# One decoder step on one core: the scheduler of the attention stage follows a model of the vector engines' queues, and the weights of a prompt tile's two heads are scaled on two engines

## The chip, the cores and the metric

One core of a Trainium2 chip. The metric is the device time of one execution in microseconds. The kernel before takes 830.26 us (median of three runs, 829.99 to 830.6).

## The reference

One inference step of one decoder layer, for a prompt of 512 tokens and a sample group of 8 sequences with 8 new tokens each (576 tokens in all) that share the weights. A combined projection (1024 to 3584 columns) feeds two groups of 8 heads of 64: retention with group norm and gate, and dilated window attention. Then one output projection, a gated feed-forward with a short convolution (2816 wide), residuals and norms.

```python
proj = _rmsnorm(x, norm1_w) @ w_in
rq, rk, rv, rg, aq, ak, av = jnp.split(proj, points, axis=-1)
ro, ret_s = _retention(rq, rk, rv, ret_s0)
ro = jax.nn.silu(rg) * groupnorm(ro)
k_all, v_all = concat([win_k, ak]), concat([win_v, av])
ao = _dilated_attention(aq, pos, k_all, v_all, k_start)   # softmax over (128,1),(512,4),(2048,16)
x = x + concat([ro, ao]) @ w_out
ua, ub = jnp.split(_rmsnorm(x, norm2_w) @ w_up, [D_FF], axis=-1)
x = x + (jax.nn.silu(causal_conv(ua)) * ub) @ w_down
y = _rmsnorm(x, normf_w)
```

The prompt has no cached keys; each sample sequence has 1024 cached rows, of which the kernel reads 768.

## The kernel before, in words

**Tiles.** Activations are kept transposed, 128 features by 576 tokens. A weight chunk is 128 output columns by up to 8 blocks of 128 inputs. Each is split by ScalarE into a rounded part (`whi`, L219) and by VectorE into the rest (`wlo`, L229), so that three products of fast matmuls give nearly full precision. A *dense step* is one such block: six matmuls of 288 columns (L254), into a PSUM tile `d`. There are two `d` tiles, and four smaller PSUM tiles `m`.

**Stages.** Load and norm; retention, with the input projection beside it (to about 150 us); attention, again with the input projection beside it (150 to 334 us); then output projection and feed-forward, dense steps only.

**The order of the work.** `Merge` writes the instruction streams of all engines in one pass, while the kernel is built. Each part of the work is a Python generator, which issues some instructions and then yields how long TensorE is taken, how long it wants to rest before its next piece, and how much of its budget it has used. `Merge` keeps a clock of TensorE's work. It resumes the generator that is due, those without a budget first, then the one that is furthest behind its budget; if none is due, the clock jumps. The rests are fixed numbers, written by hand. Each engine then executes its instructions in the order in which they were issued.

**The generators of the attention stage.**
- `in_proj` (budget 130 us): for each of the 28 column blocks it takes a `d` tile, issues its eight dense steps, and adds `in_post`, which evicts `d` on VectorE (L527 to L563). The last four blocks are retention's gates; their activation (L529) is ScalarE's, with a table load of its own, and the product with the retention result `roT` (L533) is POOL's, VectorE's for the last.
- `attn_prompt` and `attn_unit`: four head pairs, four query tiles each. A tile: the queries rounded and split (L756 to L760); scores of the two heads (L769, L771) into two `m` tiles; bias and running minimum on VectorE (`s`, L779); exponential and sum on ScalarE (L786); a reciprocal on VectorE (L789); the weights of both heads scaled on POOL (L791); transposes (L797), their evictions (`pt`, L801), and the products with the values (L810).
- `attn_sample` and `unit`: eight units of four sequences. Keys are transposed (L883) and copied by VectorE and ScalarE (`kt`, L884); POOL copies the new keys to their end (L982); scores (L893) go to a `d` tile in two halves of 512 and 264 columns, of which only the second needs the new keys; bias (L900), exponential (L905), reciprocal and scaling on VectorE (L907, L908, L910); transposes into another `d` tile (L916, L917), evictions (`spt`, L920, L921), products (L928), a copy (`ob`, L937), a transpose (L943) and two copies into `aoT` (L946).
- `mix_split` rounds and splits each finished block of `aoT` and `roT` for the output projection (L1017, L1019).

**Room in PSUM.** `room(n)` lets a generator wait until n of the four `m` tiles are free by its own count; `give(n)` frees them when the eviction has been issued, not when it is done. `d` tiles are taken without a question. The pools make the instructions wait for real, whatever the scheduler believes.

Of the kernel before, what the change touches and what calls it, by code (L numbers as in the profile page):

```python
# [94 lines left out]

class Merge:
# [7 lines left out]
    def __init__(self):  # L104
        self.clock, self.live, self.n = 0.0, [], 0

# [3 lines left out]
    def add(self, gen, left=None, delay=0.0):  # L110
        self.n += 1
        self.live.append({"g": gen, "left": left, "vt": self.floor(), "at": self.clock + delay, "n": self.n,
                          "stuck": False})

    def run(self, until=None):
        while self.live and not (until and until()):
            free = [e for e in self.live if not e["stuck"]]
            assert free, "every stream waits"
            ok = [e for e in free if e["at"] <= self.clock]
            if ok:  # L120
                e = min(ok, key=lambda e: (e["left"] is not None, e["vt"] if e["left"] else e["at"], e["n"]))
            else:
                e = min(free, key=lambda e: (e["at"], e["n"]))
                self.clock = e["at"]
            try:
# [21 lines left out]
def decoder_step(ctx, tc, a):  # L147
    nc = tc.nc
    pe, dve, act, pool, sp = nc.tensor, nc.vector, nc.scalar, nc.gpsimd, nc.sync
# [12 lines left out]
    def room(n):  # L162

        while held[0] + n > 4:
            yield None
        held[0] += n

    def give(n):
        held[0] -= n

    def dtile():
        return psd.tile([P, 1024], F32, name="d", tag="d")
# [155 lines left out]
    mg = Merge()  # L328
# [193 lines left out]
    def in_post(m, ps):  # L522
        sec, hp = m // 4, m % 4
        y = tok(ps)
        if sec == 3:
            t = atp.tile([P, T], F32, name="t3", tag="t6", bufs=1)
            dve.tensor_mul(t, y, rstd_b)  # L527
            yield 0.0, 800.0
# [6 lines left out]
        elif sec < 4:  # L535
# [4 lines left out]
            dve.tensor_mul(t, y, kds.pop(hp) if sec == 1 else rstd_b)  # L540
            if m in first:
                evac.append(m)
# [10 lines left out]
        else:  # L553
            r = A.setdefault(hp, {})
            t = atp.tile([P, T], F32, name=f"t{sec}", tag=f"t{sec}", bufs=1 if sec == 6 else 2)
            if sec == 4:
                dve.scalar_tensor_tensor(t, y, -(DH ** -0.5), rstd_b, op0=OP.mult, op1=OP.mult)  # L557
                yield 0.0, 2300.0
# [3 lines left out]
            else:  # L562
                dve.tensor_mul(t, y, rstd_b)  # L563
                yield 0.0, 1700.0
# [11 lines left out]
    def in_proj():  # L576
        for m in IN_ORDER:
# [3 lines left out]
            else:  # L581
                while hp > 1 and (sec < 3 and ret_done[0] < hp - 1 or sec > 3 and used.get(hp - 2, 0) < 6):
                    yield None
                ps = dtile()
# [159 lines left out]
    def attn_unit(hp, i):  # L744
# [111 lines left out]
    def attn_sample():  # L856
# [31 lines left out]
        def unit(u):  # L888
            hp, g = units[u]
            ps = dtile()  # L890
# [4 lines left out]
            for x in range(4):  # L895
# [5 lines left out]
                                     op1=OP.min, accum_out=c[:, 0:1])  # L901
            if g == 1 and hp < 3:
# [10 lines left out]
            yield 0.0, 1100.0  # L913
            ps = dtile()
# [6 lines left out]
            act.copy(pt[:, 3:7].rearrange("p j q -> p (j q)"), ps[:, 384:KEYS + P])  # L921
            yield 0.0, 2200.0
# [65 lines left out]
    mg.add(in_proj(), 130.0e3)  # L988
# [13 lines left out]
    rpx.close()  # L1002

# [18 lines left out]
    mg.run()  # L1022
    mid.close()
# [308 lines left out]
```

## Time and profile before

| | |
|---|---|
| median of 3 runs | 830.26 us |
| the profiled execution | 830.02 us |
| its span, first to last instruction | 828.2 us |
| TensorE busy | 809.3 us (98%) |
| VectorE, ScalarE, POOL busy | 413.4 (50%), 294.4 (36%), 148.0 us (18%) |
| granted TensorE clock, mean | 0.997 |
| DMA | 128.67 MB, 155 GB/s over the span |

Busy TensorE is not TensorE at its peak: the end of a matmul is modelled, and matmuls overlap in the record, so a short wait can lie inside a busy stretch. An idle row names who ended the wait. A row of a group gives the busy time, the mean of one instruction in ns, and the idle time ahead of it. Names like `s` or `d` are the program's tiles, without their numbers.

### The profile page before, as it was taken

How to read it: one execution, taken by the hardware profiler on the slowest of the kernel's cores; microseconds unless marked ns; L12 is line 12 of the kernel's file. 1: busy time of each engine (PE TensorE's matmuls, PEld its weight loads, DVE VectorE, ACT ScalarE, POOL GpSimd, SP SyncE). 2: the span in 40 equal slices, each digit the busy share in tenths (PEclk: the TensorE clock that was granted, in tenths of full speed). 3: DMA queues.
4: the chain of work that ended last, by engine and by line, in shares of the span. 5: the costliest groups of instructions: out<-in, count | busy, mean ns of one | idle time of the engine just before them, and what ended most of it. 6: DMA issues, size and time to landing. Idle time of an engine off the chain costs nothing.

```text
span 828.2 us, 15913 instructions
## 1 busy us (share of the span) xinstructions
PE 809.3 (98%) x6559; PEld 772.3 (93%) x6559; DVE 413.4 (50%) x792; ACT 294.4 (36%) x503; POOL 148.0 (18%) x240
## 2 busy tenths in 40 slices
PE   7999999999999999999999999999999999999995
PEld 5999999887887888999999999999999999999995
DVE  4664555665546566743545545432245545443333
ACT  5422222454535567433223323311123323332222
POOL 1321202111110213032122322100012322310111
PEclk9999999999999999999999999999999999999998
DMA  9354753678786863456255554443334455543213
GB/s 265 105 175 115 213 173 101 184 210 226 213 254 185 228 177 91 111 185 197 77 179 178 178 187 160 124 137 91 96 99 161 145 153 179 172 160 93 71 52 115
DMA packets 179798, 128.67 MB, mean 155 GB/s; under 512 B 14976, under 2 KB 176400, under 8 KB 179213
## 3 DMA queue, kind: packets, MB, share of 16 engines
q1 hardware_dynamic: 178573, 93.75, 40.4%
q10 hardware_dynamic: 928, 33.63, 11.3%
q8 instruction: 52, 0.85, 0.4%
q0 software_dynamic: 224, 0.28, 0.1%
q14 instruction: 21, 0.17, 0.1%
HBM read 121.52 MB, written 39.66 MB: 195 GB/s over the span
## 4 chain that ended last, share of the span: by engine, by line
PE 93%; ACT 3%; DVE 1%; issue 1%; DMA 1%; POOL 0%; SPq 0%; ACTq 0%; DVEq 0%
PE d L254 74%; PE m L883 2%; PE d L451 2%; PE m L928 1%; PE d L893 1%; PE m L810 1%; PE m L797 1%; PE m L496 1%; PE m L1222 1%; PE px L254 1%; PE m L666 1%; DMA wraw<-in_w_in_dram 1%; ACT s L786 1%; PE m L630 1%; PE px L410 1%
## 5 line engine op out<-in xcount | busy, mean ns | idle before, releaser
L219 ACT ACTIVATE whi<-wraw 128x1024 fp32r<-128x1024 f32 (+2 forms) x114 | 110.5, 970 | 369.2 <-issue 182.6
L229 DVE TENSOR_TENSOR wlo<-wraw,whi 128x1024 fp32r<-128x1024 f32 (+2 forms) x114 | 127.1, 1115 | 121.7 <-ACT whi L219 118.9
L254 PE MATMUL d<-bhi,whi 128*128 128x288 f32 x768 | 172.7, 306 | 1.2 <-DVE t L557 1.2
L254 PE MATMUL d<-bhi,wlo 128*128 128x288 f32 x768 | 164.2, 295 | 0.0
L254 PE MATMUL d<-blo,whi 128*128 128x288 f32 x768 | 163.9, 295 | 0.0
L254 PE MATMUL d<-hhi,whi 128*128 128x288 f32 x704 | 151.0, 296 | 0.0
L254 PE MATMUL d<-hlo,whi 128*128 128x288 f32 x704 | 150.8, 296 | 0.0
L254 PE MATMUL d<-hhi,wlo 128*128 128x288 f32 x704 | 150.7, 296 | 0.0
L254 PEld LDWEIGHTS d<-bhi,whi 128*128 128x128 f32 x768 | 121.7, 189 | 6.3 <-issue 3.1
L254 PEld LDWEIGHTS d<-bhi,wlo 128*128 128x128 f32 x768 | 123.3, 188 | 0.0
L254 PEld LDWEIGHTS d<-blo,whi 128*128 128x128 f32 x768 | 123.2, 188 | 0.0
L254 PEld LDWEIGHTS d<-hhi,whi 128*128 128x128 f32 x704 | 113.5, 189 | 0.1
L254 PEld LDWEIGHTS d<-hhi,wlo 128*128 128x128 f32 x704 | 113.5, 189 | 0.0
L254 PEld LDWEIGHTS d<-hlo,whi 128*128 128x128 f32 x704 | 113.5, 189 | 0.0
L1130 DVE TENSOR_TENSOR ue<-d,rstd_b 128x512 f32<-128x512 f32 x22 | 15.2, 691 | 74.5 <-PE d L254 74.5
L1149 POOL TENSOR_TENSOR g<-g,cv 128x512 f32<-128x512 f32 x20 | 25.8, 1289 | 142.2 <-DVE g L1146 136.7
L791 POOL TENSOR_SCALAR s<-s,sc 128x128 f32<-128x128 f32 (+3 forms) x32 | 17.3, 549 | 140.5 <-DVE sc L789 125.9
L1046 POOL TENSOR_TENSOR acc<-acc,sq 128x576 f32<-128x576 f32 x13 | 20.9, 1611 | 104.2 <-ACT sq L1045 104.2
L1135 POOL COPY cout<-ue 128x2 f32<-128x2 f32 x22 | 5.7, 260 | 137.6 <-DVE ue L1130 137.6
L884 ACT COPY kt<-m 128x384 f32<-128x384 f32 x32 | 15.3, 479 | 38.4 <-PE m L883 36.2
L883 PE MATMUL m<-ident,kc 128*128 128x128 f32 x192 | 27.4, 277 | 0.8 <-DVE sc L779 0.7
L884 DVE COPY kt<-m 128x384 f32<-128x384 f32 x32 | 17.8, 556 | 19.4 <-PE m L883 19.0
(269 smaller groups left out, 1027.3 us busy)
## 6 DMA issues: line engine op xcount, KB each, us to landing
wraw<-in_w_up_dram SPq DMA_DIRECT2D x44, 512.0 KB, 4.7
wraw<-in_w_in_dram SPq DMA_DIRECT2D x26, 512.0 KB, 3.8
kc<-in_cache_win_k_dram SPq DMA_DIRECT2D x32, 256.0 KB, 4.8
vc<-in_cache_win_v_dram SPq DMA_DIRECT2D x32, 256.0 KB, 3.2
wraw<-in_w_down_dram SPq DMA_DIRECT2D x16, 384.0 KB, 4.0
wraw<-in_w_down_dram SPq DMA_DIRECT2D x16, 320.0 KB, 3.2
kc<-in_cache_win_k_dram SPq DMA_DIRECT2D x64, 64.0 KB, 3.4
vc<-in_cache_win_v_dram SPq DMA_DIRECT2D x64, 64.0 KB, 3.3
```

The source lines that it names most:

```text
L219: act.activation(split[i][0][:, c], raw[i][:, c], AF.Copy)
L229: dve.tensor_sub(lo[:, c], raw[i][:, c], f32(hi[:, c]))
L254: pe.matmul(ps[:, C0 + s * H2:C0 + (s + 1) * H2], wt[:, rows[k] if rows else k - k0], x[k][:, s * H2:(s + 1) * H2], start=first and k == k ...
L410: pe.transpose(ps[:, s], xn[:r, j, k * P:(k + 1) * P], ident[:r, :r])
L451: pe.matmul(ps[i][:, C0 + s * H2:C0 + (s + 1) * H2], wt[:, k], x[k][:, s * H2:(s + 1) * H2], start=k == 0 and wt is hi and x is xhis, stop ...
L496: pe.transpose(p1[:, j * P:(j + 1) * P], src[:, j * P:(j + 1) * P], ident)
L791: pool.tensor_scalar(s[:, :n], s[:, :n], c[:, 2:3], 1.0, op0=OP.mult, op1=OP.mult)
L883: pe.transpose(ps[:, j * P:(j + 1) * P], K[u, x][:, 3 * w + j], ident)
L884: (act.copy if w else dve.tensor_copy)(kt[:, w * 384:w * 384 + 384], ps[:, :384])
L1046: pool.tensor_tensor(acc, acc, sq, op=OP.add)
L1130: dve.tensor_mul(u[:, 2:NP + 2], ya[:, :NP], rstd_b[:, :NP])
L1149: eng.tensor_tensor(g[:, :NP], g[:, :NP], c[:, :NP], op=OP.mult)
```

## The change

`Queues` keeps, for VectorE, ScalarE and POOL, a modelled time at which each would be done with all that was issued to it: a fixed part and a part per element for each instruction. `Engine` wraps the three engines, so that each instruction is noted there. In the attention stage (`follow`):
- a generator other than `in_proj` is not due again before the latest modelled end of what it just issued, plus 150 ns, whatever its own rest says;
- `give(n)` frees `m` tiles at that modelled end, and `room` waits for it;
- a `d` tile is taken only when the last but one has been read, by the model (`dgive`, `droom`).

Apart from the scheduler, the scaling of the weights of a prompt tile's second head goes to VectorE, the first head's stays on POOL, and the rest behind it is shorter.

```diff
+class Queues:
+    COST = {"dve": (130.0, 1.1), "act": (150.0, 0.87), "pool": (250.0, 1.0)}
...
+    def note(self, name, op, out):
+        base, each = self.COST[name]
+        n = math.prod(out.shape[1:])
+        if name == "pool" and op == "tensor_tensor":
+            each = 2.4
+        t = max(self.clock[name], self.now) + base + n * each
+        self.clock[name] = t
+        self.end = max(self.end, t)
...
             self.clock += c[0]
             e["at"] = self.clock + c[1]
+            if self.follow and not e["dense"]:
+                e["at"] = max(e["at"], self.queues.end + 150.0)
...
     def room(n):
-        while held[0] + n > 4:
-            yield None
+        while True:
+            while freed and freed[0][0] <= mg.clock:
+                held[0] -= freed.pop(0)[1]
+            if held[0] + n <= 4:
+                break
+            yield (0.0, max(freed[0][0] - mg.clock, 10.0)) if freed else None
         held[0] += n
...
     def give(n):
-        held[0] -= n
+        if mg.follow:
+            freed.append((queues.end, n))
+            freed.sort()
+        else:
+            held[0] -= n
...
+    def dgive(ps):
+        read[id(ps)] = queues.end
...
+    def droom():
+        while mg.follow and len(large) > 1:
+            t = read.get(id(large[-2]))
+            if t is not None and t <= mg.clock:
+                break
+            yield None if t is None else (0.0, max(t - mg.clock, 10.0))
...
-        for ps, s, c in S:
-            pool.tensor_scalar(s[:, :n], s[:, :n], c[:, 2:3], 1.0, op0=OP.mult, op1=OP.mult)
-        yield 0.0, 2.5 * n + 300.0
+        for eng, (ps, s, c) in zip((pool, dve), S):
+            eng.tensor_scalar(s[:, :n], s[:, :n], c[:, 2:3], 1.0, op0=OP.mult, op1=OP.mult)
+        yield 0.0, 1.25 * n + 500.0
...
-    mg.add(in_proj(), 130.0e3)
+    mg.add(in_proj(), 130.0e3, dense=True)
...
     mg.run(lambda: fin_ret)
     rpx.close()
+    mg.follow = True
```

`dgive(ps)` stands behind each instruction that reads a `d` tile for the last time, `yield from droom()` ahead of each `dtile()` of the input projection and of the sample's units. The stage up to the end of retention is issued as before. `order` rows of the changed kernel carry its own line numbers: L328 is L254 of before, L876 L797, L889 L810, L962 L883, L973 L893, L998 and L999 L916 and L917, L1011 L928, L1026 L943, and every instruction of the three wrapped engines has L131.

**Place 1: TensorE's order at the first head pair's last prompt tile.** Before, from the key transposes behind the scores of the sample's unit (which stand a few rows earlier) to the transposes of its weights:

```order
L883 MATMUL m<-ident,kc 128x128 x6
L254 MATMUL d<-bhi,whi 128x288 x2
L254 MATMUL d<-blo,whi 128x288 x2
L254 MATMUL d<-bhi,wlo 128x288 x2
L810 MATMUL m<-pt,n_1724 64x128 x8
L883 MATMUL m<-ident,kc 128x128 x6
L254 MATMUL d<-bhi,whi 128x288 x2
L254 MATMUL d<-blo,whi 128x288 x2
L254 MATMUL d<-bhi,wlo 128x288 x2
L916 MATMUL d<-ident,ss 128x128 x6
L917 MATMUL d<-ident,ss 128x128
```

and now:

```order
L962 MATMUL m<-ident,kc 128x128 x6
L973 MATMUL d<-kt,qb_404 32x512 x4
L973 MATMUL d<-kt,qb_404 32x264 x4
L570 MATMUL m<-ident,t_2230 128x128 x4
L571 MATMUL m<-ident,t_2230 128x128
L962 MATMUL m<-ident,kc 128x128 x6
L876 MATMUL m<-ident,s 128x128 x8
L998 MATMUL d<-ident,ss 128x128 x6
L999 MATMUL d<-ident,ss 128x128
```

Three dense steps stood between these groups, two of them in the rows shown; now there is none between the scores and the transposes of the weights (`d` from `ss`).

ScalarE's order there, now (`s` the prompt tile's weights, `n` the next pair's value tile, `kdec` and `ka` the next pair's keys, `ss` the sample's weights):

```order
L131 COPY kt<-m 128x384
L131 ACTIVATE s,sc<-s,sc 128x512 x2
L131 COPY n_2254<-m 128x512
L131 CAST kdec<-t_1846 64x512
L131 CAST ka_2285<-t_1846 64x512
L131 ACTIVATE ss,ssc<-ss,ssc 128x776
```

The eviction of the value tile and the casts of the next pair's keys stand between the prompt's exponentials and the sample's.

**Place 2: VectorE and POOL at the last head pair's last prompt tile.** VectorE, before, from the tile's last score pass on (`s` its scores, `sc` their sums):

```order
L779 ISA s,sc<-m,pb 128x512
L779 ISA sc 128x1
L920 COPY spt<-d 128x384
L789 RECIPROCAL sc<-sc 128x1 x2
L527 TENSOR_TENSOR t_4208<-d,rstd_b 128x576
L801 COPY pt<-m 128x512
L229 TENSOR_TENSOR wlo<-wraw,whi 128x1024
```

and now, from the eviction of a dense tile (`t`) behind its score passes on:

```order
L131 TENSOR_TENSOR t_4147<-d,rstd_b 128x576
L131 COPY kt<-m 128x384
L131 TENSOR_TENSOR wlo<-wraw,whi 128x1024
L131 RECIPROCAL sc<-sc 128x1 x2
L131 TENSOR_SCALAR s<-s,sc 128x512
```

The reciprocals stood ahead of the next split of weights (`wlo`) and now stand behind it. That split needs `whi`, and ScalarE's queue there is now: copy of `kt`, table load, the tile's two exponentials, `whi`, table load. POOL, before:

```order
L791 TENSOR_SCALAR s<-s,sc 128x384 x2
L982 COPY kt<-t_3178 128x8 x4
L533 TENSOR_TENSOR roT<-roT,t_4106 128x576
L791 TENSOR_SCALAR s<-s,sc 128x512 x2
L533 TENSOR_TENSOR roT<-roT,t_4208 128x576
```

and now:

```order
L131 TENSOR_TENSOR roT<-roT,t_3954 128x576
L131 TENSOR_SCALAR s<-s,sc 128x512
L131 COPY kt<-t_3214 128x8 x4
L131 TENSOR_TENSOR roT<-roT,t_4147 128x576
L131 MEMSET ue_4348 128x2
```

The copies of the new keys (`kt`) stood ahead of the last tile's scaling and now stand behind it.

**Place 3: the end of the attention stage.** TensorE, before, the last rows up to the last transpose of the stage:

```order
L928 MATMUL m<-n_3740,spt 32x128 x4
L254 MATMUL d<-bhi,whi 128x288 x2
L254 MATMUL d<-blo,whi 128x288 x2
L254 MATMUL d<-bhi,wlo 128x288 x2
L810 MATMUL m<-pt,n_3740 64x128 x8
L254 MATMUL d<-bhi,whi 128x288 x2
L254 MATMUL d<-blo,whi 128x288 x2
L254 MATMUL d<-bhi,wlo 128x288 x2
L254 MATMUL d<-bhi,whi 128x288 x2
L254 MATMUL d<-blo,whi 128x288 x2
L254 MATMUL d<-bhi,wlo 128x288 x2
L943 MATMUL m<-ident,ob 128x128
```

and now, with the first matmuls of the output projection at the end:

```order
L328 MATMUL d<-bhi,whi 128x288 x2
L328 MATMUL d<-blo,whi 128x288 x2
L328 MATMUL d<-bhi,wlo 128x288 x2
L889 MATMUL m<-pt,n_3623 64x128 x8
L998 MATMUL d<-ident,ss 128x128 x6
L999 MATMUL d<-ident,ss 128x128
L1011 MATMUL m<-vc,spt 32x128 x24
L1011 MATMUL m<-n_3623,spt 32x128 x4
L1026 MATMUL m<-ident,ob 128x128
L328 MATMUL d<-bhi,whi 128x288 x2
```

The last dense steps of the input projection now stand ahead of the last five groups of attention, none between them. VectorE, before, ahead of the last eviction `spt`:

```order
L907 RECIPROCAL ssc<-ssc 128x1
L908 TENSOR_SCALAR ss<-ss,ssc 128x776
L910 TENSOR_TENSOR ss<-ss,small 128x64
L779 ISA s,sc<-m,pb 128x512
L779 ISA sc 128x1
L779 ISA s,sc<-m,pb 128x512
L779 ISA sc 128x1
L920 COPY spt<-d 128x384
```

and now:

```order
L131 TENSOR_TENSOR blo<-aoT,bhi 128x576
L131 TENSOR_TENSOR t_4263<-d,rstd_b 128x576
L131 TENSOR_TENSOR blo<-aoT,bhi 128x576
L131 RECIPROCAL ssc<-ssc 128x1
L131 TENSOR_SCALAR ss<-ss,ssc 128x776
L131 TENSOR_TENSOR ss<-ss,small 128x64
L131 TENSOR_TENSOR roT<-roT,t_4263 128x576
L131 COPY spt<-d 128x384
```

The eviction of the last dense tile and a split now stand ahead of the sample's reciprocal and scaling, and the last product with `roT` ahead of `spt`.

## Rows read from the trace of the kernel before

**Rows 1.** Stages: busy us of each engine (instructions), clock, DMA share, GB/s.

```profile
core 0: us, PE busy (x) PEld busy (x) DVE busy (x) ACT busy (x) POOL busy (x), PEclk, DMA share, GB/s
...
150.00:334.00 184.00, 179.98 (x1796) 155.80 (x1796) 108.01 (x277) 100.64 (x237) 29.13 (x76) 1.00 0.71 199
334.00:400.00 66.00, 66.00 (x500) 65.80 (x498) 34.38 (x52) 23.07 (x29) 12.99 (x10) 1.00 0.53 157
400.00:500.00 100.00, 100.00 (x750) 99.93 (x751) 49.51 (x67) 32.44 (x40) 24.41 (x42) 1.00 0.53 168
500.00:800.00 300.00, 300.00 (x2263) 299.98 (x2262) 126.64 (x169) 84.70 (x107) 47.73 (x69) 1.00 0.42 129
```

**Rows 2.** Waits of TensorE's weight loads, 150 to 334 us: total, times, longest.

```profile
PEld d L893 <- POOL kt L982: 2.1, 3, 1.5
PEld m L797 <- POOL s L791: 1.9, 7, 0.5
PEld m L883 <- DVE sc L779: 1.7, 4, 0.9
...
PEld d L254 <- DVE t L557: 1.5, 1, 1.5
```

**Rows 3.** The page's groups of instructions: busy us, mean ns | idle us before.

```profile
L883 PE MATMUL m<-ident,kc 128*128 128x128 f32 x192 | 27.4, 277 | 0.8 <-DVE sc L779 0.7
```

**Rows 4.** The chain that ended last: start us, us, what.

```profile
159.26 0.81 PE m L883 x6
...
163.89 1.44 PE d L893 x16
...
192.17 1.02 PE m L810 x16
```

**Rows 5.** ScalarE's groups by shape, 150 to 334 us.

```profile
L884 ACT COPY kt<-m 128x384 f32<-128x384 f32 x32 | 15.3, 479 | 38.4 <-PE m L883 36.2 <-PE m L943 1.1 <-POOL s L791 0.6
L219 ACT ACTIVATE whi<-wraw 128x1024 fp32r<-128x1024 f32 x13 | 13.7, 1057 | 6.1 <-PE d L254 6.0
L905 ACT ACTIVATE ss<-ss,ssc 128x776 f32<-128x776 f32 x8 | 7.6, 946 | 4.2 <-DVE ssc L900 4.1
...
L786 ACT ACTIVATE s<-s,sc 128x512 f32<-128x512 f32 x8 | 5.7, 718 | 1.0 <-DVE sc L779 1.0
...
L499 ACT COPY n<-m 128x512 f32<-128x512 f32 x7 | 4.1, 588 | 12.6 <-PE m L496 12.6
...
L529 ACT ACT_TABLE_LOAD x3 | 3.8, 1283 | 0.1
...
L937 ACT COPY ob<-m 128x128 f32<-128x128 f32 x8 | 2.2, 270 | 2.3 <-PE m L928 2.3
L529 ACT ACTIVATE t<-t 128x576 f32<-128x576 f32 x3 | 2.1, 684 | 0.0
```

**Rows 6.** The timeline, pieces of three stretches: start us, us, what [idle before].

```profile
161.41 0.18 ACT L786 ACTIVATION_READ_ACCUMULATOR s<-s,sc 128x1 f32 x1
...
161.63 0.16 DVE L789 RECIPROCAL sc<-sc 128x1 f32<-128x1 f32 x1 [0.35 <-ACT s L786]
...
161.98 0.72 POOL L791 TENSOR_SCALAR s<-s,sc 128x128 f32<-128x128 f32 x2 [16.05 <-DVE sc L789]
...
186.13 1.67 DVE L229 TENSOR_TENSOR wlo<-wraw,whi 128x1024 fp32r<-128x1024 f32 x1 [0.79 <-ACT whi L219]
...
302.96 1.28 ACT L529 ACT_TABLE_LOAD   x1
...
304.25 0.68 ACT L529 ACTIVATE t<-t 128x576 f32<-128x576 f32 x1
```

**Rows 7.** VectorE's and POOL's groups by shape, 150 to 334 us.

```profile
L229 DVE TENSOR_TENSOR wlo<-wraw,whi 128x1024 fp32r<-128x1024 f32 x13 | 16.3, 1255 | 2.2 <-ACT whi L219 2.0
...
L563 DVE TENSOR_TENSOR t<-d,rstd_b 128x576 f32<-128x576 f32 x7 | 5.3, 754 | 5.7 <-PE d L254 5.6
L908 DVE TENSOR_SCALAR ss<-ss,ssc 128x776 f32<-128x776 f32 x8 | 5.0, 625 | 0.3
L920 DVE COPY spt<-d 128x384 f32<-128x384 f32 x8 | 4.5, 556 | 3.2 <-PE d L917 3.1
...
L982 POOL COPY kt<-t 128x8 f32<-128x8 f32 x32 | 5.5, 220 | 0.1
L791 POOL TENSOR_SCALAR s<-s,sc 128x512 f32<-128x512 f32 x8 | 5.5, 697 | 29.6 <-DVE sc L789 17.9 <-PE d L916 11.7
```

More of the change, by code (lines that the diff above doesn't have):

```diff
@@ L93, in _constants, with __init__, step, __getattr__ @@
     return {"c_ident": ident.astype(f), "c_small": small, "c_kdec": kdec, "c_pbias": pb, "c_sbias": sb.astype(f)}
+class Queues:
+    COST = {"dve": (130.0, 1.1), "act": (150.0, 0.87), "pool": (250.0, 1.0)}
+    def __init__(self):
+        self.clock = dict.fromkeys(self.COST, 0.0)
+        self.now, self.end = 0.0, 0.0
+    def step(self, now):
+        self.now, self.end = now, now
+    def note(self, name, op, out):
[6 more added lines that the diff above has]
+        self.end = max(self.end, t)
+class Engine:
+    def __init__(self, engine, name, queues):
+        self.engine, self.name, self.queues = engine, name, queues
+    def __getattr__(self, op):
+        f = getattr(self.engine, op)
+        if op == "dma_start":
+            return f
+        def call(*args, **kw):
+            r = f(*args, **kw)
+            self.queues.note(self.name, op, kw["out"] if "out" in kw else args[0])
+            return r
+        return call
 class Merge:
-    def __init__(self):
+    def __init__(self, queues):
         self.clock, self.live, self.n = 0.0, [], 0
+        self.queues, self.follow = queues, False
     def floor(self):
         return min([e["vt"] for e in self.live if e["left"] and not e["stuck"]], default=0.0)
-    def add(self, gen, left=None, delay=0.0):
+    def add(self, gen, left=None, delay=0.0, dense=False):
         self.n += 1
         self.live.append({"g": gen, "left": left, "vt": self.floor(), "at": self.clock + delay, "n": self.n,
-                          "stuck": False})
+                          "stuck": False, "dense": dense})
     def run(self, until=None):
@@ L124, in run @@
                 self.clock = e["at"]
+            self.queues.step(self.clock)
             try:
@@ L148, in decoder_step @@
     nc = tc.nc
-    pe, dve, act, pool, sp = nc.tensor, nc.vector, nc.scalar, nc.gpsimd, nc.sync
+    pe, sp = nc.tensor, nc.sync
+    queues = Queues()
+    dve, act, pool = (Engine(e, n, queues) for e, n in ((nc.vector, "dve"), (nc.scalar, "act"), (nc.gpsimd, "pool")))
     ctx.enter_context(tc.manual_schedule())
@@ L162, in room @@
     def room(n):
-        while held[0] + n > 4:
-            yield None
+        while True:
[4 more added lines that the diff above has]
+            yield (0.0, max(freed[0][0] - mg.clock, 10.0)) if freed else None
         held[0] += n
+    freed = []
     def give(n):
-        held[0] -= n
+        if mg.follow:
[3 more added lines that the diff above has]
+            held[0] -= n
+    large, read = [], {}
+    def dgive(ps):
[6 more added lines that the diff above has]
+            yield None if t is None else (0.0, max(t - mg.clock, 10.0))
     def dtile():
-        return psd.tile([P, 1024], F32, name="d", tag="d")
+        large.append(psd.tile([P, 1024], F32, name="d", tag="d"))
+        return large[-1]
     def f32(ap):
@@ L326, in halves @@
         return [(h2, slice(h2 * 64, h2 * 64 + 64)) for h2 in range(2)]
-    mg = Merge()
+    mg = Merge(queues)
     xhi = big.tile([P, KD, T], F32R, name="bhi", tag="bhi", bufs=1)
@@ L527, in in_post @@
             dve.tensor_mul(t, y, rstd_b)
+            dgive(ps)
             yield 0.0, 800.0
@@ L583, in in_proj @@
                     yield None
+                yield from droom()
                 ps = dtile()
@@ L889, in unit @@
             hp, g = units[u]
+            yield from droom()
             ps = dtile()
@@ L913, in unit @@
             yield 0.0, 1100.0
+            yield from droom()
             ps = dtile()
@@ L1022, in decoder_step @@
     mg.run()
+    mg.follow = False
+    held[0] = 0
     mid.close()
```

5 lines of the change are left out of this document (added).

## The prediction

> **What bounds the kernel now.** I read the stages first, then who makes TensorE wait, then the prices. The table by stage [rows 1] shows TensorE busy without a gap from 334 to 800 us; the gap before 150 us and the one after 800 us lie in parts whose order the change leaves as it is. What the change can reach is the stage from 150 to 334 us: 180.0 of 184.0 us busy, so 4.0 us idle. There TensorE alternates between pieces of attention and steps of the dense input projection (six matmuls of 288 columns), which exist to fill its waits. Its work is the same in both kernels; so the time changes by waits alone.
>
> The waits of TensorE's weight loads in that stage [rows 2] name their causes: POOL's copies of the new keys (3 waits), POOL's scaling of the weights (7), VectorE's score passes that free PSUM (4), VectorE's eviction of a dense tile (1). A matmul's shown end is modelled: a transpose of 128 columns shows 277 ns [rows 3] where six of them take 0.81 us, 0.135 each [rows 4]. Each wait therefore hides some 0.14 us more than its idle row says. **Lost now: 4.0 + 15 x 0.14 = 6.1 us.** The ends: 4.0 (the idle alone) and 7.2 (the four rows of the weight loads, counted in full).
>
> **What the change removes.** Its scheduler holds each attention piece until a model of the three vector queues says that its inputs are there, and does not begin a dense tile before the last but one has been read. All four causes are addressed, so I let 5.7 of the 6.1 us go and keep 0.4. The order shows that the attention pieces move to later places while the dense steps go on at once, so those run out earlier. New waits come from that, and I price them at the three places shown under the change, by what stands on the queues. Ends of the ranges are the same chains with nothing and with 0.19 us for every handover.
>
> **Place 1, the first head pair's last prompt tile.** Where three dense steps stood among the groups, none stands now. From the end of the key transposes (L883) to the transposes of the sample's weights (L916) TensorE has the sample's scores, 1.44 us for both halves [rows 4], five transposes of a value tile (5 x 0.135 = 0.68), six of keys (0.81) and eight of weights (1.08): 4.0 us. ScalarE meanwhile does, in its queue's order, the key copy 0.479, two exponentials of 0.718, the value copy 0.588, two casts of 512 columns (taken as that copy, 0.588 each) and the sample's exponential 0.946 [rows 5]; VectorE then a reciprocal of 0.16 [rows 6] and the scaling 0.625 [rows 7]. Sum 5.4. **Wait 1.4 us.** The second head's scaling, now on VectorE, lies beside this: no trace of before shows 128x512 there; by the 776 columns in 625 ns it is 0.41, by POOL's 0.697 at most [rows 7]; either hides behind the two casts. I take 0.41, the same engine.
>
> **Place 2, the last head pair's last prompt tile.** POOL's copies of the sample's new keys now stand on its queue behind the scaling of the last tile's first head, and the second half of the sample's scores needs them. That scaling waits for a reciprocal on VectorE, which stands behind a weight split (L229), which waits for ScalarE's weight rounding (L219), which stands behind both exponentials and, in front of them, a table load. From the end of the key transposes: copy 0.479, table load 1.283, exponentials 2 x 0.718, rounding 1.057 [rows 5], split 1.255 [rows 7], reciprocal 0.16 [rows 6], scaling 0.697, first key copy 0.220 [rows 7]: 6.6 us. Cover on TensorE: 24 dense matmuls at 100 us / 750 = 0.133 [rows 1], 3.2 us, and the first 512 of 776 columns of scores, 0.95 of 1.44: 4.1. **Wait 2.5 us**, before the second half of the scores.
>
> **Place 3, the end of the stage.** Before, three dense steps lie among the last four groups. Now the last dense step is followed by nothing but attention, five groups in one chain. (a) VectorE has an eviction of the dense tile and a split of 576 columns (0.754 each, the split taken as the eviction), the reciprocal and the scaling: 2.3 us after the last dense matmul, against 1.02 us of TensorE work (L810): wait 1.3. (b) The pack of the transposed weights (L920) now stands on VectorE behind the last gate product, which waits for ScalarE's sigmoid-weighted gate (L529) and its table load: 0.588 + 1.283 + 0.684 on ScalarE, 0.754 + 0.556 on VectorE, 3.9 us after L810; TensorE has spent 1.3 + 7 x 0.135 of it: wait 1.6. (c) The last result (L937) must be copied, 0.27, before its transpose. **Wait 3.2 us.** The output projection behind it has three steps of 0.8 us before it needs the last attention rows, and these need two small copies, a cast and a split on VectorE, the longest of them 0.754 [rows 7]: nothing.
>
> **Handovers.** The three places have 14 of them; the rows give 0.04 us from ScalarE to VectorE and 0.19 from VectorE to POOL [rows 6]. At 0.07 as a mean: 1.0 us; from 0.6 to 2.7.
>
> **Where cost is nothing.** ScalarE loads its tables seven times in the stage instead of five, 2 x 1.283 more; two of the seven are in places 2 and 3 already, the others lie under dense steps. The 16 scalings that VectorE takes over add at most 16 x 0.41 = 6.6 us to 108 busy of 184 [rows 1]; their cover is gone only where VectorE is the last of a chain, as in place 3, where none stands. On SP the loads keep their order within each tensor, and no row of the stage shows a load as a cause.
>
> **The sum.** New: 1.4 + 2.5 + 3.2 + 1.0 = 8.1 us. Gone: 5.7. Net +2.4 us: 830.02 of the profiled execution becomes 832.4, and as the median of the runs is 0.24 us above that execution, 832.7. What a measurement of this kernel can tell from no change is about 0.2%, 1.7 us.
>
> **A rule against the trace.** A table load is followed by the next activation at once: 302.96 + 1.28, then 304.25 [rows 6]. So the sum has 1.283 for each. The Trainium skill (ScalarE: Activation LUTs, What ACT_TABLE_LOAD costs) counts for each switch of tables a drain of 1380 ns beside the same 1283; by it places 2 and 3 would each be 1.4 us longer, and the time 835.5. The row does not show the drain.
>
> **Rivals.** *A, faster:* the waits end and are not replaced. In place 2 ScalarE would have to be ahead, with the table loaded before the key copy is due, and in place 3 wait (b) would have to be covered. Then new waits are 1.4 + 1.2 + 1.6 and 0.7 of handovers, 4.9, and if the weight loads' 7.2 us are all lost now and all gone, the net is -2.3: 828.0. It decides at 6.1 us of new waits. For it: the scheduler counts 738 ns for a dense step that takes 800, so real cover is larger than it believes. Against: the chains above already use the real cover. *B, no change that can be measured:* the same chains with half of place 2 and place 3's (c) hidden, +0.85: 831.1. *C, slower still:* the two engines do not scale side by side. A weight split took 1.67 us while POOL was scaling, against 1.255 in the mean [rows 6, 7], 0.41 more. If each waits for the other, the 7 waits on the scaling stay: +1.9, 834.6. The Trainium skill (SBUF — State Buffer, Who interferes with whom) has the rule for it: a VectorE scaling may take the port pair that it shares with GpSimd for the whole instruction, and the other engine blocks; the long split agrees with the section's line on instructions with two SBUF inputs. *D, a pause after each table load,* as long as the load: 2 x 1.283 in places 2 and 3, 835.3; the activation at 304.25 speaks against it. *E, the change moves nothing that TensorE waits for:* excluded, since the dense steps go at all three places.
>
> **Chances.** Forecast 0.54, A 0.11, B 0.20, C 0.13, D 0.02, E 0. The likeliest case's own range is 831.2 (6.8 us gone, handovers at 0.04) to 834.8 (3.6 us gone). Of its 0.54, some 0.04 lie under the bound of 0.2%. Slower by over 0.2%: 0.50 + 0.13 + 0.02 = 0.65; the same 0.20 + 0.04 = 0.24; faster 0.11. To leave out no more than 2 in 10 the whole takes in C and the forecast's upper end, and reaches part of the way to A: 829.3 to 835.0.
>
> **What would show it.** Right: in the changed profile TensorE waits between the two halves of the scores (d from kt) for POOL's kt copies some 15 us before the end of the stage, and before the first output-projection step it waits for VectorE's ss, for VectorE's spt and for ScalarE's ob; the chain that ended last names ScalarE's table loads there; waits of TensorE for POOL's s and for a dense eviction are gone. Wrong: TensorE without an idle row in the last 30 us of the stage, or waits of over half a microsecond that still name POOL's s.

## The result, and the profile after

The changed kernel takes 837.92 us (median of 6 runs, 836.46 to 840.19), the kernel before, run beside it, 829.67 us (6 runs, 829.06 to 830.6): ratio 1.0101, 95% interval 1.0087 to 1.0115, so 8.25 us slower. The forecast was 832.7 us with a range up to 835.0: the sign was right, the size was not. The profiled execution of the changed kernel took 840.19 us; its span is 838.4 us.

The stages of the changed kernel, columns as in [rows 1], with the time from 322 to 346 us cut finer, and a stretch at place 1:

```profile
150.00:334.00 184.00, 178.20 (x1724) 155.46 (x1723) 108.74 (x288) 99.46 (x233) 21.56 (x60) 0.98 0.71 199
197.50:200.00 2.50, 2.47 (x13) 1.92 (x13) 1.38 (x3) 0.03 (x1) 0.00 (x0) 0.50 0.98 304
322.00:329.00 7.00, 4.35 (x34) 3.27 (x32) 2.70 (x6) 6.72 (x10) 0.99 (x2) 1.00 0.04 12
329.00:334.00 5.00, 4.83 (x21) 3.34 (x22) 2.89 (x6) 1.66 (x4) 2.60 (x5) 0.66 0.00 0
334.00:337.00 3.00, 3.00 (x27) 2.83 (x27) 0.73 (x2) 1.86 (x3) 0.00 (x0) 1.00 0.00 0
337.00:342.00 5.00, 2.02 (x29) 1.55 (x29) 3.42 (x7) 2.87 (x4) 0.10 (x1) 0.87 0.01 3
342.00:346.00 4.00, 3.61 (x59) 2.98 (x52) 0.18 (x1) 1.29 (x4) 0.10 (x1) 0.50 0.40 132
...
400.00:800.00 400.00, 400.00 (x3011) 399.72 (x3010) 177.08 (x247) 116.33 (x145) 71.83 (x110) 1.00 0.45 139
```

Read two columns, TensorE's busy time and PEclk. The stage from 400 to 800 us is as full as before [rows 1]; the loss lies in the attention stage and right behind it. TensorE is idle there for 5.80 us up to 334 and 3.4 us from 334 to 346, 9.2 us where it was 4.0 before. But the granted clock, 1.00 throughout in [rows 1], is now 0.50 in 197.5:200 (place 1), 0.66 in 329:334 (place 2) and 0.50 in 342:346 (place 3): there TensorE ran at 1.2 GHz, the lower of its two levels, for part or all of the time. Ahead of all three it had stood still.

Who TensorE waited for, 150 to 346 us (total, times, longest):

```profile
PE d L973 <- POOL kt L131: 2.8, 1, 2.8
PE d L998 <- DVE ss L131: 2.3, 2, 1.4
PE m L1011 <- DVE spt L131: 1.6, 1, 1.6
PE m L876 <- DVE n L131: 0.9, 1, 0.9
PE m L876 <- DVE kt L131: 0.5, 1, 0.5
PE m L1026 <- ACT ob L131: 0.4, 1, 0.4
PE m L570 <- DVE t L131: 0.4, 1, 0.4
PE m L962 <- ACT n L131: 0.2, 1, 0.2
```

The waits of the forecast are there by name: POOL's `kt` at place 2, `ss`, `spt` and `ob` at place 3, the chain to `ss` at place 1 (0.9 of the 2.3). The `n`, `kt` and `n` rows belong to place 1 too; the forecast did not name them. No row names POOL's `s`, and none waits for a dense tile to be freed: the four causes of [rows 2] are gone outside the three places. The 0.4 us of L570 is a new one, a wait for the data of an evicted tile.

What the waits did to the work behind them is in TensorE's own timeline (start us, us, what, idle before):

```profile
189.86 0.87 PE L962 MATMUL m<-ident,kc 128*128 128x128 f32 x6
...
197.53 1.54 PE L998 MATMUL d<-ident,ss 128*128 128x128 f32 x6 [0.92 <-DVE ss L131]
...
199.95 1.46 PE L889 MATMUL m<-pt,n 128*64 128x128 f32 x16
...
325.29 1.07 PE L973 MATMUL d<-kt,qb 128*32 128x512 f32 x8
329.14 2.14 PE L973 MATMUL d<-kt,qb 128*32 128x264 f32 x8 [2.79 <-POOL kt L131]
331.21 1.97 PE L876 MATMUL m<-ident,s 128*128 128x128 f32 x8
...
336.67 1.10 PE L889 MATMUL m<-pt,n 128*64 128x128 f32 x16
...
341.70 2.79 PE L1011 MATMUL m<-vc,spt 128*32 128x128 f32 x48 [1.60 <-DVE spt L131]
```

Six transposes took 0.87 us at 189.86 and 1.54 us at 197.53, behind a wait. Sixteen products (L889) took 1.46 us at 199.95 and 1.10 at 336.67, where the clock was 1.00. In the changed kernel's chain that ended last, the 56 products of L1011 are 3.26 us long; the run below in which TensorE was kept busy has them in 1.52 and 0.40, overlapping.

### The profile page after: what moved, and what is told of

It is laid out like the page before. It is cut to its first block, busy times and chain, and to the rows that moved or that the text cites. A ratio compares the mean times of both kernels' runs of the same rounds, so it can differ in the third digit from the quotient of the medians.

```text
span 838.4 us, 15881 instructions
## 1 busy us (share of the span) xinstructions
PE 813.9 (97%) x6559; PEld 777.0 (93%) x6559; DVE 415.8 (50%) x808; ACT 297.0 (35%) x505; POOL 140.2 (17%) x224
## 4 chain that ended last, share of the span: by engine, by line
PE 95%; ACT 2%; DVE 1%; DMA 1%; issue 0%; SPq 0%; POOL 0%; ACTq 0%; DVEq 0%; POOLq 0%
PE d L328 74%; PE m L962 3%; PE d L525 2%; PE m L1011 2%; PE m L889 1%; PE d L973 1%; PE m L876 1%; PE m L570 1%; PE m L1308 1%; PE px L328 1%; DMA wraw<-in_w_in_dram 1%; PE m L745 1%; PE px L484 1%; PE m L848 1%; PE m L709 1%; ACT s L131 1%
## 5 line engine op out<-in xcount | busy, mean ns | idle before, releaser
L131 ACT ACTIVATE whi<-wraw 128x1024 fp32r<-128x1024 f32 (+2 forms) x114 | 110.6, 970 | 367.7 <-issue 186.7
L131 DVE TENSOR_TENSOR wlo<-wraw,whi 128x1024 fp32r<-128x1024 f32 (+2 forms) x114 | 126.9, 1113 | 124.4 <-ACT whi L131 121.6
L328 PE MATMUL d<-bhi,whi 128*128 128x288 f32 x768 | 173.2, 307 | 0.0
L328 PE MATMUL d<-bhi,wlo 128*128 128x288 f32 x768 | 164.5, 296 | 0.0
L328 PE MATMUL d<-blo,whi 128*128 128x288 f32 x768 | 164.4, 296 | 0.0
L328 PE MATMUL d<-hhi,whi 128*128 128x288 f32 x704 | 150.9, 296 | 0.0
L328 PE MATMUL d<-hlo,whi 128*128 128x288 f32 x704 | 150.8, 296 | 0.0
L328 PE MATMUL d<-hhi,wlo 128*128 128x288 f32 x704 | 150.7, 296 | 0.0
L328 PEld LDWEIGHTS d<-bhi,whi 128*128 128x128 f32 x768 | 122.6, 190 | 4.6 <-issue 3.0
L328 PEld LDWEIGHTS d<-blo,whi 128*128 128x128 f32 x768 | 123.9, 189 | 0.0
L328 PEld LDWEIGHTS d<-bhi,wlo 128*128 128x128 f32 x768 | 123.7, 189 | 0.0
L328 PEld LDWEIGHTS d<-hhi,whi 128*128 128x128 f32 x704 | 113.4, 189 | 0.1
L328 PEld LDWEIGHTS d<-hhi,wlo 128*128 128x128 f32 x704 | 113.4, 189 | 0.0
L328 PEld LDWEIGHTS d<-hlo,whi 128*128 128x128 f32 x704 | 113.4, 189 | 0.0
L131 DVE TENSOR_TENSOR ue<-d,rstd_b 128x512 f32<-128x512 f32 (+1 forms) x44 | 18.1, 454 | 74.6 <-PE d L328 74.6
L131 POOL TENSOR_TENSOR g<-g,cv 128x512 f32<-128x512 f32 (+1 forms) x40 | 31.2, 802 | 142.1 <-DVE g L131 136.7
L131 POOL COPY cout<-ue 128x2 f32<-128x2 f32 (+1 forms) x44 | 30.8, 730 | 137.8 <-DVE ue L131 137.8
L131 DVE TENSOR_TENSOR xT<-d,xT 128x576 f32<-128x576 f32 x23 | 17.4, 757 | 54.5 <-PE d L328 54.5
L131 POOL TENSOR_TENSOR acc<-acc,sq 128x576 f32<-128x576 f32 x13 | 21.0, 1615 | 109.6 <-ACT sq L131 109.6
L131 DVE SCALAR_TENSOR_TENSOR cv<-ue,vec,cv 128x592 f32<-128x592 f32 x44 | 36.5, 829 | 0.8
L131 POOL TENSOR_SCALAR s<-s,sc 128x128 f32<-128x128 f32 (+3 forms) x16 | 10.2, 635 | 141.0 <-DVE sc L131 114.9
L131 ACT COPY kt<-m 128x384 f32<-128x384 f32 x32 | 15.3, 478 | 47.3 <-PE m L962 45.2
```

The lines of the kernel that those rows point to most:

```text
L131: r = f(*args, **kw)
L328: pe.matmul(ps[:, C0 + s * H2:C0 + (s + 1) * H2], wt[:, rows[k] if rows else k - k0], x[k][:, s * H2:(s + 1) * H2], start=first and k == k ...
```

## The experiments

**Theory 1:** the waits came about as priced, and what the sum missed is the clock after them. **Rivals:** the waits alone, longer than priced; rival C, VectorE and POOL slowing each other in the split scaling. A second question: which half of the edit makes the loss, the scheduler or the split?

### Keeping TensorE busy in the waits

Extra matmuls whose results nothing reads stand in front of the waiting instructions.

```diff
+        def fill(ps, c0, n):
+            for _ in range(n):
+                pe.matmul(ps[:, c0:c0 + P], ident, ident, start=True, stop=True)
...
+                if u == 7 and n0:
+                    fill(ps, 800, 12)
...
+            if u in (1, 7):
+                fill(scores, 0, 4 if u == 1 else 6)
...
+            if u == 7:
+                fill(scores, 0, 7)
...
+            if u == 7:
+                fill(scores, 0, 2)
```

> The changed kernel, with extra 128x128 matmuls of the identity put in front of the matrix instructions that wait at places 1 to 3 (12 between the two halves of the last sample unit's scores, 4 or 6 before the transposes of its weights at place 1 and 3a, 7 before its products, 2 before the last small transpose). Their results are read by nothing, so the output and every wait's cause stay as they are; only TensorE is busy while it waits. Theory 1 (about 5.5 us of the 8.2 us lost are the lower level of TensorE's clock, which is granted after the new waits): the granted clock of 341.7:345.8 rises from 0.50 to near 1.00, L1011's products take about 1.7 us again instead of 3.26, and the time is 832 to 834 us. Rival (the loss is the waits themselves, with what they delay): the waits are still sat out, the time stays 837 to 839 us. Rival (split scaling slows VectorE and POOL side by side): no change either, 837 to 839 us.

Measured: 833.79 us (833.43 to 834.73, 5 runs), ratio 1.0045 (1.0033 to 1.0057) to the kernel before. Its stage, and TensorE's rows (L1021 the products):

```profile
329.00:334.00 5.00, 5.00 (x48) 4.66 (x47) 3.06 (x6) 3.74 (x6) 0.14 (x1) 1.00 0.01 3
342.00:346.00 4.00, 4.00 (x32) 4.00 (x32) 3.93 (x7) 0.00 (x0) 0.00 (x0) 1.00 0.41 100
```

```profile
328.40 1.09 PE L876 MATMUL m<-ident,s 128*128 128x128 f32 x8
...
337.63 1.52 PE L1021 MATMUL m<-vc,spt 128*32 128x128 f32 x48
338.97 0.40 PE L1021 MATMUL m<-n,spt 128*32 128x128 f32 x8
```

With more instructions to execute, the kernel is over 4 us faster: the ratio falls from 1.0101 to 1.0045, 0.56% of 830 us or 4.6 us. The eight transposes of L876 take 1.09 us instead of 1.97. Nothing that VectorE, POOL or ScalarE must do was taken away, so the two rivals are out for this part. What remains, 3.9 us, is put down to the waits; the forecast's net was 2.4. Place 1 is filled only ahead of `ss`, and its three shorter waits (0.24, 0.88 and 0.47 us) stay. Three of the five executions show a mean granted clock of 0.998 (833.4 to 833.8 us), two 0.994 (834.4 and 834.7): the filling does not keep the clock up everywhere each time.

### One place at a time

The same edit at place 3 alone, and at place 2 alone.

> The changed kernel with the unused identity matmuls at place 3 alone (6 before the transposes of the last unit's weights, 7 before its products, 2 before the last transpose). Theory 1 (the lower clock after the waits makes up what the sum missed, place by place): the products take 1.7 us again instead of 3.26, the granted clock there returns to 1.00, and 2 to 3 of the 4.1 us that the filling of all three places gave back come back: 835 to 836 us; places 1 and 2 keep a clock of 0.66 to 0.97 behind their waits. Rival (one fall at place 2 is what pulls the clock down to the end): filling place 3 changes nothing there, 837 to 838 us.

Measured: 837.21 us (836.87 to 837.75, 4 runs), ratio 1.0096 (1.0079 to 1.0113).

> The changed kernel with the 12 unused identity matmuls at place 2 alone, between the two halves of the last unit's scores. Theory 1: what follows place 2 runs at the full clock, 1 to 2 us come back, 836 to 837 us, and place 3 still shows a clock near 0.5 behind its own waits. Rival (one fall at place 2 pulls the clock down to the end): place 3 runs at 1.00 too, 834 us.

Measured: 834.31 us (833.15 to 836.02, 4 runs), ratio 1.0063 (1.0044 to 1.0081). Place 3 alone filled:

```profile
329.00:334.00 5.00, 5.00 (x23) 3.98 (x22) 2.50 (x5) 2.52 (x4) 1.58 (x2) 0.50 0.00 0
342.00:346.00 4.00, 4.00 (x64) 3.80 (x57) 2.10 (x5) 2.37 (x4) 0.10 (x1) 1.00 0.74 221
```

and place 2 alone:

```profile
329.00:334.00 5.00, 4.97 (x35) 3.79 (x35) 3.40 (x6) 2.53 (x4) 2.49 (x4) 1.00 0.01 3
334.00:337.00 3.00, 2.04 (x24) 1.62 (x22) 1.84 (x4) 1.84 (x4) 0.00 (x0) 1.00 0.00 0
337.00:342.00 5.00, 2.69 (x63) 2.19 (x63) 1.72 (x4) 2.46 (x5) 0.20 (x2) 1.00 0.27 94
```

Each filling lifts the clock where it is. The times do not follow the expected split: by the ratios place 3 gave 0.4 us, not told apart from nothing by the intervals, and place 2 gave 3.2. With place 3 filled, the profiled execution has the lower level through the whole of 329:334, the changed kernel's only in part (0.66); this may hide part of the gain. And in the second trace the waits at place 3 are all there (TensorE busy 2.04 of 3 and 2.69 of 5 us), with the clock at 1.00. So either the fall at place 2 had pulled the clock down at place 3 too, or place 3's waits bring it down in some executions only.

> The changed kernel with the unused identity matmuls at place 1 (4) and place 2 (12), and none at place 3, whose three waits (1.4, 1.6 and 0.4 us) stay. If the fall at place 2 is what brings the clock down at place 3 as well, as the run with place 2 alone filled suggests (its place 3 stood at 1.00), all of what the filling of the three places gave back comes back: 833.5 to 834.5 us, and place 3 shows 1.00. If place 3's own waits bring it down, its stretch shows about 0.5 again and the time is 835 to 836.5 us.

Measured: 835.4 us (832.2 to 835.96, 6 runs), ratio 1.0064 (1.0052 to 1.0076). The median hides two groups: the executions whose mean granted clock was 0.997 and 0.998 took 832.2 and 833.4 us, the four at 0.993 took 835.2 to 836.0. The profiled one is of the first kind, with the three waits of place 3 there and the clock up:

```profile
PE m L1019 <- DVE spt L131: 1.6, 1, 1.6
PE d L1006 <- DVE ss L131: 1.4, 1, 1.4
PE m L876 <- DVE n L131: 0.9, 1, 0.9
PE m L876 <- DVE kt L131: 0.5, 1, 0.5
PE m L1034 <- ACT ob L131: 0.4, 1, 0.4
```

```profile
334.00:337.00 3.00, 1.40 (x37) 1.14 (x38) 1.23 (x2) 1.46 (x3) 0.10 (x1) 1.00 0.12 16
```

So the clock falls in some executions of this kernel and not in others, for about 3 us of difference. Where it fell in the four others no trace shows: place 3 was left unfilled, but place 1 kept its waits for `n` and `kt`, and behind place 1's waits the clock fell in the run with place 2 alone filled (0.50 in 196:202, with places 2 and 3 at 1.00). Between the two readings this run does not decide. The first fits all three traces: place 3 fell where place 2 had fallen, and stayed up in the two in which place 2 was filled. That waits at the end of the stage can bring the clock down with no fall shortly before them is shown further down, by the scheduler alone, with a longer first wait. How much each place costs by itself is thereby not settled; the sum of the three is.

### What a wait costs by itself

In the kernel before, in the stage where TensorE has no gap, eight waits of graded length on a chain of small VectorE copies that nothing else reads:

```diff
+        n = WAITS.get(key[1], 0) if key[0] == "up" else 0
+        if n:
+            pe.matmul(ps[:64, :P], wsc, ident, start=True, stop=True)
+            for _ in range(n):
+                dve.tensor_copy(wsc, ident[:, :64])
+            pe.matmul(ps[:64, :P], wsc, ident, start=True, stop=True)
...
```

> The kernel before with eight waits put into the stretch from 400 to 700 us, where TensorE has no gap: in front of every second tile of the first feed-forward projection TensorE must wait for a chain of 1, 4, 8, 12, 2, 16, 6 and 22 small VectorE copies (64 columns, which nothing else reads); two small extra matmuls begin and end each. Theory 1: behind the longer of them (1.5 us and more) TensorE's matmuls of 288 columns take about twice their 0.133 us for some time, so these waits cost more than their length; with copies of 0.16 to 0.2 us the waits sum to 11 to 14 us, and with some 1.5 to 2 us more behind each of the four longest the time is 847 to 853 us; the short ones leave the clock at 1.00. Rival (a wait costs its length alone): 841 to 845 us and a granted clock of 1.00 throughout.

Measured: 859.87 us (858.4 and 861.35). TensorE behind two of the waits (L260 is the dense step's matmul), and the stretch behind the second in the columns of [rows 1]:

```profile
465.17 0.43 PE L254 MATMUL d<-ident,wsc 128*64 128x128 f32 x2 [1.89 <-DVE wsc L253]
465.53 0.54 PE L260 MATMUL d<-hhi,whi 128*128 128x288 f32 x2
465.91 0.42 PE L260 MATMUL d<-hlo,whi 128*128 128x288 f32 x2
466.17 0.42 PE L260 MATMUL d<-hhi,wlo 128*128 128x288 f32 x2
...
493.94 0.43 PE L254 MATMUL d<-ident,wsc 128*64 128x128 f32 x2 [2.81 <-DVE wsc L253]
494.30 0.85 PE L260 MATMUL d<-hhi,whi 128*128 128x288 f32 x2
494.95 0.68 PE L260 MATMUL d<-hlo,whi 128*128 128x288 f32 x2
495.43 0.68 PE L260 MATMUL d<-hhi,wlo 128*128 128x288 f32 x2
```

```profile
495.50:497.50 2.00, 2.00 (x10) 2.00 (x10) 1.96 (x4) 0.09 (x1) 0.99 (x2) 0.50 1.56 524
```

The waits of 0.29, 0.52, 0.97, 1.43 and 1.89 us cost their length: the clock stayed at 1.00. Behind those of 2.81, 3.73 and 5.10 us a pair of dense matmuls takes 0.48 us from start to start instead of 0.26, until the clock returns; against the same number of pairs behind the 0.29 wait that is 1.5, 1.5 and 2.1 us, 5.2 in all. The profiled execution adds up: 829.3 (the kernel before beside it) + 16.7 of waits + 5.2 + 8 x 0.8 for the extra matmuls (at the 0.29 wait the next dense matmul starts 1.08 us after the first extra one, 0.79 without the wait) = 857.6, measured 858.4. The expected time was too low because a wait grew by 0.23 us with each copy (a copy's own row shows 0.195) and every place had the 0.8; the rival's clock of 1.00 throughout is refuted.

### Which part of the edit

The scheduler alone, both heads scaled on POOL:

> The changed kernel with both heads' prompt weights scaled on POOL again and the old rest after it (2.5n + 300): the scheduler's part of the change alone. Theory 1 (waits at places 1 to 3, made by the new order, and the lower clock after them): the place 2 and 3 waits come from the order, so most of the loss stays: 834 to 837 us, with the granted clock again under 0.7 in the stretch after the last unit's waits. Rival (the scaling on two engines at once costs the time): 829 to 831 us. Rival (the scheduler alone costs it, and the split gives some back): 838 us or more.

Measured: 832.96 us (830.13 to 835.15, 11 runs), ratio 1.0034 (1.0023 to 1.0046): under the interval expected by theory 1 and over the first rival's. The wait for POOL's `kt` at place 2 is not there. The waits at the end are (2.1 us for `ss`, then 0.65 and 0.40), and behind them the clock is low, with TensorE full and the clock at 1.00 in the 10 us ahead of them:

```profile
334.00:337.00 3.00, 2.49 (x48) 2.27 (x52) 0.45 (x1) 0.58 (x1) 0.00 (x0) 0.51 0.54 175
```

The split alone, in the kernel before:

> The kernel before with only the scaling split over POOL and VectorE, and the new rest after it (1.25n + 500): no model of the queues. Theory 1 (the order makes the waits): the order shifts only where the shorter rest lets a step come earlier; some of the waits for POOL go, some steps run into VectorE: 829 to 833 us, with no wait over 2 us on POOL's copies of the last unit's keys. Rival (the split itself, by VectorE and POOL slowing each other, costs the time): 835 to 838 us.

Measured: 833.33 us (832.86 to 834.58, 6 runs), ratio 1.0041 (1.0029 to 1.0053), just over what theory 1 expected; in the profiled execution the clock stays at 1.00, so this loss is of waits. Alone, the scheduler costs 0.34% and the split 0.41%; together 1.01%, more than their sum, so neither half makes the loss by itself. The split's edit has two halves, the engine of 16 scalings and the rest that the scheduler counts behind them, so each was run alone.

```diff
-        for ps, s, c in S:
-            pool.tensor_scalar(s[:, :n], s[:, :n], c[:, 2:3], 1.0, op0=OP.mult, op1=OP.mult)
+        for eng, (ps, s, c) in zip((pool, dve), S):
+            eng.tensor_scalar(s[:, :n], s[:, :n], c[:, 2:3], 1.0, op0=OP.mult, op1=OP.mult)
         yield 0.0, 2.5 * n + 300.0
```

> The kernel before with the scaling of two heads split over POOL and VectorE, and the old rest of 2.5n + 300 after it: the order of every engine's other work stays as it was, only 16 scalings change their engine. Theory (the split costs through the order that the shorter rest makes, not through the two engines): the chains of the prediction give 6.9 us of waits where the kernel before has 6.2, so 830 to 831.5 us, with the clock at 1.00. Rival C (VectorE and POOL hold each other up): a POOL scaling takes 0.9 us and more where it took 0.697, the waits for POOL's s stay, 833 us or more.

Measured: 830.95 us (829.54 to 833.07, 11 runs), ratio 1.0011 (0.9999 to 1.0024). POOL's row answers to [rows 7]:

```profile
L791 POOL TENSOR_SCALAR s<-s,sc 128x512 f32<-128x512 f32 x4 | 3.3, 834 | 30.4 <-DVE sc L789 18.2 <-PE d L916 12.2
...
L791 DVE TENSOR_SCALAR s<-s,sc 128x512 f32<-128x512 f32 x4 | 2.0, 507 | 0.1
```

The other half, `yield 0.0, 1.25 * n + 500.0` behind two scalings on POOL:

> The kernel before with the shorter rest of 1.25n + 500 after the scaling, both heads still scaled on POOL: the other half of the split's edit, which moves pieces of attention to earlier places. Theory (the loss of 3.4 us with the split alone comes from this order): the chains give 8.9 us of waits where the kernel before has 6.2: 832 to 834 us. Rival C: without the second engine no loss, 829 to 831 us.

Measured: 833.3 us (832.77 to 833.51, 5 runs), ratio 1.0042 (1.003 to 1.0055), the whole loss of the split. So the two engines cost at most 2 us and perhaps nothing; the order that follows from the shorter rest costs 3.5, spread over waits of up to 0.9 us, for VectorE's score passes (L883, 1.8 us in three) and POOL's `s` (1.3 in two) above all. Part of it is the clock: in the profiled execution, behind two waits of 0.90 and 0.74 us close together at 200 to 202 us, it is 0.50 in 204:206. The split's profiled execution has the same two waits and kept 1.00. Four of the five executions here show 0.994; the one at 0.997 took 832.8 us, so most of the loss is the waits.

### Other orders

One number of the changed kernel, and one of the kernel before: `mg.add(in_proj(), ...)` with another budget.

> The changed kernel with one number changed: the share of the dense input projection in the merge is 150.0e3 where it was 130.0e3, which shifts where its steps fall among the attention pieces. By the same chains as in the prediction the waits of the stage sum to some 7.4 us where the changed kernel has 9.6, with one wait of about 1.9 us and none between the halves of the last scores. Theory 1: 832 to 835 us, the clock low behind that one wait alone. Rival (the loss is spread through the stage by the scaling on two engines and the held pieces, not in the places): 837 us or more.

Measured: 833.39 us (830.97 to 835.67, 5 runs), ratio 1.0045 (1.0024 to 1.0066), within theory 1. The wait for `kt` between the halves of the scores is gone; the longest, 1.7 us, is now for a key load, which was not expected. Nor did the clock do what theory 1 said: behind that wait, at 244 us, it stayed at 1.00, and it fell to 0.50 at place 1 (197 to 199 us), whose four waits are the changed kernel's.

> The kernel before with one number changed: the share of the dense input projection in the merge is 120.0e3 where it was 130.0e3, so that its steps fall a little later among the attention pieces. The chains give 5.1 us of waits where the kernel before has 6.2, none over 1 us, so the clock stays: 828 to 829.5 us. If a wait of over 2 us appears all the same, or the dense steps run past the end of the stage, 830 us or more.

Measured: 829.58 us (828.39 to 830.29, 11 runs), ratio 0.9995 (0.9987 to 1.0004): no difference that can be measured, and just over what was expected.

> The kernel before with the split over POOL and VectorE, the old rest, and 120.0e3 for the input projection. The chains give 5.1 us of waits where the kernel before has 6.2, the longest 1.4: 828 to 829.5 us. Rival C (the engines hold each other up): 831 us or more.

Measured: 830.08 us (829.52 to 832.01, 11 runs), ratio 1.0009 (1.0 to 1.0018): between the two expectations, and no gain either. No kernel tried beats the one before.

## Why the prediction was right, and where it was not

**What bounds the kernel** was read rightly: the stages from 400 us on did not move, and the new waits stand at the three places, in the forecast's order and with its causes. **What the change removes** too: of TensorE's 9.2 idle us all but 0.5 stand at the three places, and the old causes are gone from the rest.

**The step that failed** is in the first part: "Its work is the same in both kernels; so the time changes by waits alone." The work is the same, its speed is not. The sum had no term for the granted clock, and that term is the largest of all: 4.6 us by the run with the three places filled. Without it the forecast of +2.4 us is near, and at the low end: the two executions with places 1 and 2 filled in which the clock stayed up lie 2.4 and 3.6 us above the kernel before beside them, the run with three places filled 3.9, and the idle rows of the profiled execution give 9.2 - 4.0 = 5.2. In the stage that the change reaches, the longest wait of before is 1.5 us [rows 2], and the clock is 1.00 [rows 1]: no row showed what happens behind a longer one. A forecast that makes a wait of 2.5 us, and three waits in a row at the end, needed a bound for it from both sides like any other operation that the trace does not show; the sum took the one end, nothing, without saying so. The upper end was short by its own rule as well: with 0.19 us for each of the 14 handovers and 3.6 us gone it is 836.5 where 834.8 stands, and the measured 837.92 lies above that too.

**The places, against their terms.** Place 2: 2.79 us, forecast 2.5. Place 3: 1.39 + 1.60 + 0.39 = 3.4, forecast 1.3 + 1.6 + 0.27. Place 1: 0.24 + 0.88 + 0.47 + 0.92 = 2.5, forecast 1.4; here the term was mis-sized. VectorE's timeline there:

```profile
194.64 0.68 DVE L131 TENSOR_TENSOR kdec<-t,kdec 64x512 fp32r<-64x512 f32 x1
195.34 0.56 DVE L131 COPY kt<-m 128x384 f32<-128x384 f32 x1
...
195.41 0.19 ACT L131 ACTIVATION_READ_ACCUMULATOR ss<-ss,ssc 128x1 f32 x1
...
195.93 0.69 DVE L131 TENSOR_TENSOR ka<-t,ka 64x512 fp32r<-64x512 f32 x1
196.65 0.16 DVE L131 RECIPROCAL ssc<-ssc 128x1 f32<-128x1 f32 x1
```

The sample's exponential and its sum were done at 195.60, but the reciprocal began at 196.65: VectorE had a split of 0.68 us, a copy and another split ahead of it. The forecast followed ScalarE's queue and gave VectorE only the reciprocal and the scaling. The handovers' 1.0 us cannot be told from the rest; with them the forecast of the new waits is 8.1 us, and the rows of the three places give 8.7.

**The chain** of the changed kernel names two of ScalarE's table loads there, as forecast, at 322.71 and 338.41 us (a table load has no tile's name):

```profile
338.41 1.28 ACT L131
339.69 0.01 issue
339.70 0.69 ACT t L131
```

**The rivals.** A (faster) fell, since all its waits are there. B fell. C (the engines do not scale side by side) fell as priced, since no wait for POOL's `s` is left in the changed kernel; a smaller effect is there. With the order kept, a POOL scaling of 512 columns takes 0.834 us beside VectorE's 0.507, and 0.697 in the kernel before [rows 7]. That is 0.14 longer, over the four of this width 0.55 us of POOL's time. By the Trainium skill (SBUF — State Buffer, Who interferes with whom) the engine that comes second may stand for the other's whole instruction, here 0.51; the mean shows about a quarter of that. (The split of 1.67 us that the forecast took for C ran beside POOL's scaling only until 186.73; then POOL copied keys.) D (a pause after a table load) fell: the activation started 0.01 us behind it, in the rows above as in [rows 6]; the drain in the Trainium skill (ScalarE: Activation LUTs, What ACT_TABLE_LOAD costs) shows in no run.

**Not settled:** the share of each place in the clock's 4.6 us, and why the clock falls in some executions only. One of the changed kernel's six executions shows a mean granted clock of 0.996, as the kernel before does (0.996 to 0.998), and took 837.05 us; the other five show 0.987 to 0.991 and took 836.5 to 840.2. For that one the clock explains little, and its loss has no cause on record; the executions of the kernel before spread by some 4 us (828.4 to 832.6) at those same clocks. The Trainium skill (TensorE: Matmul & The Clock Gate, What's actually happening) calls the number of matmuls at the lower level run-variable for one and the same kernel; it says so of a kernel's start. The six executions at 832.2 to 836.0 us show the like for the middle of one.

## What to carry to other kernels

When an edit reorders work on a nearly full TensorE, add a second price to every new wait that is longer than those the trace shows, or stands close to another: the work right behind it at half speed, 1.5 to 2.1 us behind each of the long ones measured here. It is paid in some executions and not in others. Follow every queue that feeds the waiting instruction, not only the slowest one. And an order from a scheduler's rests is fragile: one rest, with no instruction changed, cost 3.5 us here, most of it in waits from 171 to 313 us, with none behind. So look at the whole stage, and in a changed order like this one's at its end first, where the filler work has run out.

## What the runs showed that was not expected

- The same waits (1.4, 1.6 and 0.4 us within 6 to 8 us) stood ahead of 1.2 GHz and of 2.4 GHz: the lower level is there in the profiled execution of the changed kernel (0.50 in 342:346), the upper in two other profiled kernels (1.00).
- Extra work made the kernel faster: 31 unused matmuls of the identity gave back about half of the loss.
- A single wait of 1.89 us left the clock up and one of 2.81 us did not, in one execution; both numbers are of that execution alone.
- Short waits close together were followed by the lower level where a single longer one was not: two of 0.90 and 0.74 us in the run with the shorter rest, four of 0.24 to 0.92 us at place 1, against single ones of 1.73 us (for the key load) and 1.89 us.
